# First four projection blocks of a hybrid decoder layer as float32 products of x times G, with rstd and the shift applied at eviction

## Chip, cores and metric

The kernel runs on one core of a Trainium2 chip. The metric is the device time of one execution in microseconds (us); lower is better. Engines are named as in the profile: PE is TensorE (matrix products; PEld its weight loads), DVE is VectorE, ACT is ScalarE, POOL is GpSimd, SP is SyncE. SP and POOL issue the transfers from and to HBM here.

## What is computed

One decoder layer over 2048 positions of width 1024. The part that matters here is the start: the modulation from the condition c, the modulated RMS norm, and the first columns of the combined input projection.

```python
cond = jax.nn.silu(c)
mod = (cond @ w_ada[l] + b_ada[l])[:, None, :]
sh1, sc1, g1, sh2, sc2, g2 = jnp.split(mod, N_MOD, axis=-1)

h = rms_norm(x, norm1_g[l]) * (1 + sc1) + sh1
proj = h @ w_in[l]
gq, gk, gv, gr, glr, aq, ak, av = jnp.split(proj, split_at, axis=-1)
```

Behind it come a chunked gated linear attention (from gq, gk, gv, gr, glr), a dilated softmax attention (from aq, ak, av), the output projection with a gated residual, and a second sub-layer with an up-projection, a causal convolution of width 3, a SwiGLU and a down-projection. All inputs are float32.

With G = norm1_g * (1 + sc1) and rstd the reciprocal root of the mean square of a position, h = x * G * rstd + sh1. G and sh1 belong to a column of x, rstd to a position. So h @ w = rstd * ((x * G) @ w) + sh1 @ w, where the last term is one number per output column.

## The kernel before

**Layout.** Positions are worked in four chunks (NCH) of T = 512. Within a chunk, activations lie transposed: 8 tiles (KD) of 128 channels by 512 positions. A block of weights w_ch is 128 x 1024: eight 128 x 128 pieces, one per k.

**Products.** Most products are "split": both operands are cut into a rounded part (hi) and the rest (lo), of type float32r, and `mm3` (L298) makes three products per piece: hi by hi (L304), hi of the weights by lo (L305), lo of the weights by hi (L306). Weights are loaded raw and split by `wslot` (L229): a cast on ACT (L238) gives hi, a subtraction on DVE (L239) gives lo. The raw tiles have two buffers, hi and lo four each.

**The start** (`run`, L1080). `ada_setup` loads c and the tables and makes silu(c) in `cond` (up to a factor of 2). `load_x(0)` loads the eight tiles of x. Sums of squares (L424, L429, L1091) go through a product with a matrix of ones (L443, plain float32), and L445 and L446 make rstd. The loop at L1096 then does, for each k: load scale block KD + k and shift block k of w_ada (L356; each 128 x 1024, in one or two pieces); for k < 4 load and split one of the blocks in FIRST = (0, 1, 2, 3); multiply each w_ada block with cond and sum it along its row (L360), which gives 128 values of `mod`; turn a scale into a column of G1 (L369); make one piece of the normalised input h0 by `norm_mod1`: x * G * rstd (L463, DVE), plus shift with rounding to hi (L465, ACT), and the rest as lo (L467, DVE). After the loop the four blocks are multiplied with `mm3` for each block and k (L1110 to L1112) into four PSUM tiles `done[b]`. These come from the pool `psg`, which has four.

**What follows.** `proj(0)` goes through ORDER0: g0 to g3 evict the four done blocks (`glaqk`, L518: ACT copies from PSUM with a factor, L521, then a store); the next entry, V0, is the first other work on TensorE (`av(0)`, L559, its products at L579 of 272 columns, L304 to L306 in the rows). A planner (`plan`, L248) lists all later weight blocks in order of use; `weights` (L287) loads and splits them up to three ahead. From there TensorE's work is a single stream: projections of four chunks, then the mixing of chunk c beside the up- and down-projections.

**What sets the order.** Each engine works its own queue in order. The program is written in the order above; the scheduler may place an instruction of an engine ahead of others that it doesn't depend on, and it does so at the start. Transfers of the start are issued by SP (`dq` while `planned` is false), later ones by POOL. `tie` and `after` add a dependence of a load on an instruction by hand. Tiles with a tag and a number of buffers make a load wait until the buffer's last reader is done.

Of the kernel before, what the change touches and what calls it, by code (L numbers as in the profile page):

```python
# [19 lines left out]
P = 128  # L20
T = 512
NCH = 4
KD = 8
# [4 lines left out]
FIRST = (0, 1, 2, 3)  # L28
# [84 lines left out]


def along(a, na, b, nb):

    acc = 0.0
    done = object()
    for _ in b:
        acc += na / nb  # L120
        while acc >= 1.0:
            acc -= 1.0
            if next(a, done) is done:
                acc = -1e9
        yield
    for _ in a:
        pass


def chain(*gs):  # L130
    for g in gs:
        yield from g


class K:
# [90 lines left out]
                y=d(f"y{c}", [8, P, T]), x1=d(f"x1{c}", [8, P, T])))  # L226


    def wslot(self, src, n=1024, spare=None):  # L229
        nc = self.nc  # L230
        raw = self.wraw.tile([P, 1088], F32, name="wraw")
        self.dq.dma_start(raw[:, :n], src)  # L232
        if spare is None:
            hi = self.whi.tile([P, 1088], F32R, name="whi")
            lo = self.wlo.tile([P, 1088], F32R, name="wlo")
        else:
            hi, lo = spare[:, 0:1024], spare[:, 1024:2048]
        nc.scalar.copy(hi[:, :n], raw[:, :n])  # L238
        nc.vector.tensor_tensor(lo[:, :n], raw[:, :n], hi[:, :n].bitcast(F32), op=ALU.subtract)  # L239
        return hi, lo  # L240

    def wblock(self, src, k, m, spare=None):
        hi, lo = self.wslot(src, k * m, spare)
        vh = hi[:, :k * m].rearrange("p (k m) -> p k m", k=k)
        vl = lo[:, :k * m].rearrange("p (k m) -> p k m", k=k)
        return [(vh[:, i], vl[:, i]) for i in range(k)]
# [96 lines left out]
    def soon(self, inst, n=20):  # L343
# [4 lines left out]
                break  # L348
        self.tc.add_manual_dep(inst.ins, mm.ins.name, mybir.DependencyInfo(mybir.DependencyClass.Sync, mybir.DependencyReason.DATA))

    def ada(self, b, raws):

        nc = self.nc
        n = 1024 // len(raws)
        for i, raw in enumerate(raws):
            ld = nc.sync.dma_start(raw, self.A["w_ada"][b][:, i * n:(i + 1) * n])  # L356
        yield
        m = self.mod[:, b:b + 1]
        for i, raw in enumerate(raws):
            self.last = nc.vector.tensor_tensor_reduce(raw, raw, self.cond[:, i * n:(i + 1) * n], 0.5, m if i else self.ba[:, b:b + 1], ALU.mult, ALU.add, m)  # L360
        self.ada_end(b)

    def ada_end(self, b):
# [107 lines left out]
    def proj(self, c, hs, hook=None, done=()):  # L471
        nc, A, D = self.nc, self.A, self.D[c]
# [3 lines left out]
        def stage(tag=None):  # L476
            if tag:
                return self.up.tile([P, T], F32, name="stg", tag=tag)
            return self.xp.tile([P, T], F32, name="stg", tag="x")

        def chan(b):
            w = self.weights("w_ch", b)
            ps = self.pg()
            self.mm3(ps, w, hs)
            return ps
# [30 lines left out]
            yield  # L516

        def glaqk(b):  # L518
            ps = done[b] if b in done else chan(b)
            s = stage()  # L520
            nc.scalar.activation(s, ps, AF.Copy, scale=0.125 if b < 2 else 1.0)  # L521
            self.dq.dma_start(D["gq" if b < 2 else "gk"][b % 2], s)
            yield

# [68 lines left out]
        def stores(g):  # L593

            for i, _ in enumerate(g):
                if late and i == 0:
                    next(late.pop(), None)
                yield

        ops = dict(W=wide, V=av, g=glaqk, q=qk)  # L600
        order = ORDER if c else ORDER0
        if put_off:
# [477 lines left out]
    def run(self):  # L1080
        self.ada_setup()
        self.scratch()
        self.x1, self.h2, self.tail = {}, {}, ()
        self.planned = False
        xs = self.load_x(0)
        acc = None
        for k in range(5):
            acc = self.square(acc, xs[k])
        sqs = [self.tmp.tile([P, T], F32, name="sq", bufs=3) for _ in range(5, KD)]
        for sq, x in zip(sqs, xs[5:]):  # L1090
            self.nc.scalar.activation(sq, x, AF.Square)  # L1091
        rstd = {0: self.norm_end(acc, more=sqs)}
        h0, ws, done = [], {}, {b: self.pg() for b in FIRST}
        spare = self.at.tile([P, 2048], F32R, name="w0", tag="kt", bufs=2)
        ring = self.at.tile([P, 2048], F32, name="ring", tag="kt", bufs=2)
        for k in range(KD):  # L1096
            big = [self.at.tile([P, 1024], F32, name="wada", tag="big", bufs=4)]
            pair = [self.gp.tile([P, T], F32, name="wada", tag=t) for t in ("ghi", "glo")] if k < 5 else [ring[:, (k - 5) * 1024:(k - 4) * 1024] if k < 7 else self.at.tile([P, 1024], F32, name="wada", tag="v4", bufs=1)]
            gs = [self.ada(KD + k, big), self.ada(k, pair)]
            for g in gs:  # L1100
                next(g)
            if k < len(FIRST):
                b = FIRST[k]
                ws[b] = self.wblock(self.A["w_ch"][b], KD, P, spare if k == 3 else None)
            for g in gs:
                next(g, None)
            if k == GATE:
                self.gate_ins = self.last
            h0.append(self.norm_mod1(xs[k], k, rstd[0], self.G1, self.mod[:, 0:8]))
        for b in FIRST:  # L1110
            for k in range(KD):
                self.mm3(done[b], ws[b][k:k + 1], h0[k:k + 1], k == 0, True)  # L1112
        self.consts()

        def src(c):
            def f(k):
                t = self.tmp.tile([P, T], F32, name="sq", bufs=3)
                ld = self.dq.dma_start(t, self.A["xT"][c, k])
                if c == 1:
                    self.after(ld)  # L1120
                return t
            return f

        self.wleft, self.wready, self.wpos = list(self.plan()), [], 0
        self.planned = True
        hs = [h0]

        def begin(c):
            hs.append(self.norm_mod(src(c), rstd[c], self.G1, self.mod[:, 0:8]))

        def proj(c):
            yield from self.proj(c, hs.pop(), (lambda: begin(c + 1)) if c < 3 else None, () if c else done)

        def stats(c):

            acc = None
            xs = [src(c)(0)]
            yield
            for k in range(KD):
                if k + 1 < KD:  # L1140
                    xs.append(src(c)(k + 1))
                yield
# [79 lines left out]
```

## Time and profile before

| what | us |
|---|---|
| median of 3 runs | 2595.93 |
| lowest, highest | 2593.44, 2597.0 |
| the profiled execution | 2592.85 |
| its span | 2591.1 |
| TensorE busy in the span | 2552.5 |
| DVE, ACT, POOL busy | 1930.3, 1276.8, 443.5 |

The profiled execution is one of its own; its span is the time from its first to its last instruction, and 1.75 us lie around it. Rows of the profile give the line, the engine, the operation, the tile written and the tiles read, the shape, and the count. In the rows of products, "128*128" is the stationary operand and "128x512" the streamed one; a row says f32 for float32 and float32r operands alike. A product's recorded length overlaps the next one's, so the cost of a product in a row of products is the distance of their starts.

### The profile page before, as it was taken

Reading aid. Unit: us, or ns where it says so; the run is one execution under the profiler, and the core shown is the slowest. Engines: PE = TensorE matmul, PEld = TensorE weight load, DVE = VectorE, ACT = ScalarE, POOL = GpSimd, SP = SyncE. Lnnn points to the kernel's source line nnn. Section 1 sums busy time; section 2 is a strip of 40 time slices with the busy share of each in tenths; the row PEclk is TensorE's granted clock in tenths of the full one; section 3 lists DMA queues with packets and bytes.
Section 4 is the critical chain, followed back from the end, with each engine's and each line's share of the span. In section 5 each row is a group of like instructions: output and inputs, shape, how many; then the busy total and the mean of one; then the engine's idle time right before and its main releaser. Section 6 shows DMA issues by size and latency. Waiting matters only on the chain.

```text
span 2591.1 us, 46836 instructions
## 1 busy us (share of the span) xinstructions
PE 2552.5 (99%) x18142; PEld 2099.2 (81%) x18142; DVE 1930.3 (74%) x4091; ACT 1276.8 (49%) x2626; POOL 443.5 (17%) x816
## 2 busy tenths in 40 slices
PE   6999999999999999999999999999999999999999
PEld 4888888788788888887888888878888888788887
DVE  8678877867688777677977777689777775766665
ACT  4556655766464544454545545346444553433332
POOL 2343432323210000022000000310000003100001
PEclk8999999999999999999999999999999999999999
DMA  8776764756532333355334343743443435422222
GB/s 316 245 235 221 233 214 167 237 178 210 213 111 95 123 129 129 124 197 184 108 110 133 125 131 125 253 139 114 125 145 125 141 102 191 155 98 98 98 97 83
DMA packets 163810, 404.93 MB, mean 156 GB/s; under 512 B 19154, under 2 KB 61572, under 8 KB 162308
## 3 DMA queue, kind: packets, MB, share of 16 engines
q0 software_dynamic: 88128, 308.59, 35.0%
q1 hardware_dynamic: 75460, 93.35, 11.4%
q8 instruction: 143, 2.34, 0.4%
q14 instruction: 79, 0.65, 0.1%
HBM read 338.95 MB, written 62.91 MB: 155 GB/s over the span
## 4 chain that ended last, share of the span: by engine, by line
PE 78%; issue 1%; DVE 1%; DMA 0%; ACT 0%; POOL 0%; POOLq 0%; DVEq 0%; ACTq 0%
PE psg L304 22%; PE psg L305 22%; PE psg L306 22%; PE psa L849 2%; PE psa L829 2%; PE psa L953 2%; PE psa L679 1%; PE psa L948 1%; PE psa L864 0%; PE psa L752 0%; PE psa L751 0%; PE psa L968 0%; PE psa L756 0%; PE psa L778 0%; DVE sq L463 0%
## 5 line engine op out<-in xcount | busy, mean ns | idle before, releaser
L304 PE MATMUL psg<-hhi,whi 128*128 128x512 f32 x1992 | 780.3, 395 | 10.2 <-ACT hhi L465 5.8
L305 PE MATMUL psg<-hlo,whi 128*128 128x512 f32 x1992 | 782.6, 394 | 6.4 <-DVE hlo L467 6.2
L306 PE MATMUL psg<-hhi,wlo 128*128 128x512 f32 x1992 | 780.0, 392 | 0.7 <-DVE wlo L239 0.7
L238 ACT CAST whi<-wraw 128x1024 fp32r<-128x1024 f32 (+1 forms) x391 | 410.4, 1051 | 471.2 <-PE psg L305 367.8
L239 DVE TENSOR_TENSOR wlo<-wraw,whi 128x1024 fp32r<-128x1024 f32 (+1 forms) x391 | 478.4, 1224 | 185.4 <-ACT whi L238 179.7
L304 PEld LDWEIGHTS psg<-hhi,whi 128*128 128x128 f32 x1992 | 374.3, 188 | 95.8 <-ACT hhi L465 9.8
L305 PEld LDWEIGHTS psg<-hlo,whi 128*128 128x128 f32 x1992 | 375.3, 188 | 85.9 <-DVE hlo L467 8.9
L306 PEld LDWEIGHTS psg<-hhi,wlo 128*128 128x128 f32 x1992 | 375.4, 188 | 80.5 <-issue 1.7
L304 PE MATMUL psg<-ghi,whi 128*128 128x512 f32 x744 | 295.0, 398 | 0.1
L305 PE MATMUL psg<-glo,whi 128*128 128x512 f32 x744 | 292.3, 393 | 0.9 <-DVE glo L998 0.9
L306 PE MATMUL psg<-ghi,wlo 128*128 128x512 f32 x744 | 291.5, 392 | 0.7 <-DVE wlo L239 0.7
L232 POOL DMA_DIRECT2D wraw<-in_w_up_dram x176 | 93.2, 530 | 983.0 <-DVE wlo L239 863.6
L1072 DVE SCALAR_TENSOR_TENSOR x<-psg,mod,x 128x512 f32<-128x512 f32 x192 | 143.4, 749 | 118.1 <-PE psg L306 115.5
L304 PE MATMUL psg<-whi,hhi 128*128 128x512 f32 (+2 forms) x512 | 171.4, 342 | 2.2 <-ACT stg L548 2.1
L306 PE MATMUL psg<-whi,hlo 128*128 128x512 f32 (+2 forms) x512 | 172.8, 341 | 0.0
L305 PE MATMUL psg<-wlo,hhi 128*128 128x512 f32 (+2 forms) x512 | 172.6, 339 | 0.1
L304 PEld LDWEIGHTS psg<-ghi,whi 128*128 128x128 f32 x744 | 139.5, 188 | 34.5 <-issue 5.3
L306 PEld LDWEIGHTS psg<-ghi,wlo 128*128 128x128 f32 x744 | 139.7, 188 | 30.6 <-DVE wlo L239 1.1
L305 PEld LDWEIGHTS psg<-glo,whi 128*128 128x128 f32 x744 | 139.8, 188 | 30.3 <-issue 1.9
L839 ACT ACTIVATE big<-big,nm 128x256 f32<-128x256 f32 (+1 forms) x256 | 122.4, 480 | 33.3 <-DVE nm L854 33.2
L1027 ACT ACTIVATE y<-psg,tables_sb 128x512 f32<-128x512 f32 x176 | 135.8, 774 | 4.5 <-PE psg L306 3.3
L1028 DVE SCALAR_TENSOR_TENSOR y<-psg,tables_sb,y 128x511 f32<-128x511 f32 x176 | 131.0, 745 | 3.7 <-ACT y L1027 3.6
(253 smaller groups left out, 3618.5 us busy)
## 6 DMA issues: line engine op xcount, KB each, us to landing
wraw<-in_w_up_dram POOLq DMA_DIRECT2D x176, 512.0 KB, 3.5
wraw<-in_w_down_dram POOLq DMA_DIRECT2D x88, 512.0 KB, 3.5
wraw<-in_w_ch_dram POOLq DMA_DIRECT2D x44, 512.0 KB, 4.2
v<-v SPq DMA_DIRECT2D x68, 256.0 KB, 5.4
wada<-in_w_ada_dram POOLq DMA_DIRECT2D x64, 256.0 KB, 4.9
wraw<-in_w_tokw_dram POOLq DMA_DIRECT2D x32, 512.0 KB, 4.2
wraw<-in_w_out_dram POOLq DMA_DIRECT2D x32, 512.0 KB, 4.4
sq<-in_xT_dram POOLq DMA_DIRECT2D x48, 256.0 KB, 4.6
```

The costliest lines, as they stand in the source:

```text
L232: self.dq.dma_start(raw[:, :n], src)
L238: nc.scalar.copy(hi[:, :n], raw[:, :n])
L239: nc.vector.tensor_tensor(lo[:, :n], raw[:, :n], hi[:, :n].bitcast(F32), op=ALU.subtract)
L304: nc.tensor.matmul(ps, wh, hh, start=first and k == 0, stop=False, skip_group_check=shared)
L305: nc.tensor.matmul(ps, wh, hl, start=False, stop=False, skip_group_check=shared)
L306: self.lastmm = nc.tensor.matmul(ps, wl, hh, start=False, stop=k == n - 1, skip_group_check=shared)
L829: nc.tensor.matmul(at(i, hh, z), q[H[hh], i * P:(i + 1) * P], key(H[hh], i, z), start=True, stop=True, skip_group_check=True)
L839: nc.scalar.activation(t[:, lo:hi], t[:, lo:hi], AF.Exp, bias=nm[:, hh, g, i:i + 1], scale=2.0 ** -(h + 1), accum_out=dn[:, hh, g, i:i + 1])
L849: nc.tensor.transpose(ps[:n, i * P:(i + 1) * P], part(S[hh], i), self.C("id"))
L1027: nc.scalar.activation(y, ps, AF.Identity, bias=self.cb[:, b:b + 1], scale=self.cw[:, 2, b:b + 1])
L1028: nc.vector.scalar_tensor_tensor(y[:, 1:], ps[:, :T - 1], self.cw[:, 1, b:b + 1], y[:, 1:], op0=ALU.mult, op1=ALU.add)
L1072: nc.vector.scalar_tensor_tensor(x1, ps, self.mod[:, 40 + cb:41 + cb], x1, op0=ALU.mult, op1=ALU.add)
```

## The change

The first four blocks are multiplied in plain float32, without a split, with g = x * G as the streamed operand (ACT, scale = G1 column) and the raw weights. The loop goes over k outside and the blocks inside. rstd is multiplied in at the eviction (DVE, from PSUM), and the shift's part, sh1 @ w, comes from 32 products of one column each into one PSUM tile `ps`; ACT adds it as a bias. The normalised input h0 is still made, for all later blocks.

The loads are issued in another order: the first scale block, then x, then a w block and a scale block in turn, the other scale blocks, and then all shift blocks. The tiles that they land in change with that. The first two weight loads of the planner are tied to the last scale step (`held`).

```diff
-    def wslot(self, src, n=1024, spare=None):
+    def wslot(self, src, n=1024):
...
-        self.dq.dma_start(raw[:, :n], src)
...
+        ld = self.dq.dma_start(raw[:, :n], src)
+        if self.held:
+            self.tie(ld, self.held.pop())
+        hi = self.whi.tile([P, 1088], F32R, name="whi")
+        lo = self.wlo.tile([P, 1088], F32R, name="wlo")
...
         def glaqk(b):
-            ps = done[b] if b in done else chan(b)
             s = stage()
-            nc.scalar.activation(s, ps, AF.Copy, scale=0.125 if b < 2 else 1.0)
+            scale = 0.125 if b < 2 else 1.0
+            if b in done:
+                nc.vector.tensor_tensor(s, done[b], self.rstd0, op=ALU.mult)
+                nc.scalar.activation(s, s, AF.Identity, scale=scale, bias=self.shw[:, b:b + 1])
+            else:
+                nc.scalar.activation(s, chan(b), AF.Copy, scale=scale)
...
+        scales = [self.ada_load(KD, [raw("wada")])]
         xs = self.load_x(0)
+        two = self.at.tile([P, 2048], F32, name="w0", tag="kt", bufs=2)
+        ws = [two[:, 0:1024], two[:, 1024:2048]] + [self.whi.tile([P, 1088], F32, name="whi")[:, 0:1024] for _ in range(2)]
+        for k in range(1, KD):
+            if k <= len(FIRST):
+                nc.sync.dma_start(ws[k - 1], self.A["w_ch"][FIRST[k - 1]])
+            scales.append(self.ada_load(KD + k, [raw("wada")]))
...
+            shifts.append(self.ada_load(k, raws))
...
         for k in range(KD):
-            big = [self.at.tile([P, 1024], F32, name="wada", tag="big", bufs=4)]
...
-                ws[b] = self.wblock(self.A["w_ch"][b], KD, P, spare if k == 3 else None)
...
+            self.ada(*scales[k])
+            g = self.at.tile([P, T], F32, name="xg", tag=("pt", "s16", "stage")[(k > 4) + (k > 6)], bufs=5 if k < 5 else 2)
+            nc.scalar.activation(g, xs[k], AF.Copy, scale=self.G1[:, k:k + 1])
+            for i, b in enumerate(FIRST):
+                self.lastmm = nc.tensor.matmul(done[b], ws[i][:, k * P:(k + 1) * P], g, start=k == 0, stop=k == KD - 1, skip_group_check=True)
+        self.hist.append((4 * KD, self.lastmm))
+        self.held = [self.last, self.last]
+        h0 = []
+        for k in range(KD):
+            self.ada(*shifts[k])
             if k == GATE:
                 self.gate_ins = self.last
             h0.append(self.norm_mod1(xs[k], k, rstd[0], self.G1, self.mod[:, 0:8]))
-        for b in FIRST:
+        ps = self.pa()
+        for i in range(len(FIRST)):
             for k in range(KD):
-                self.mm3(done[b], ws[b][k:k + 1], h0[k:k + 1], k == 0, True)
+                nc.tensor.matmul(ps[:, i:i + 1], ws[i][:, k * P:(k + 1) * P], self.mod[:, k:k + 1], start=k == 0, stop=k == KD - 1)
+        self.shw = self.const.tile([P, 4], F32, name="shw")
+        nc.vector.tensor_scalar(self.shw[:, 0:2], ps[:, 0:2], 0.125, None, op0=ALU.mult)
+        nc.vector.tensor_copy(self.shw[:, 2:4], ps[:, 2:4])
         self.consts()
```

More of the change, by code (lines that the diff above doesn't have):

```diff
@@ L226, in scratch @@
                 y=d(f"y{c}", [8, P, T]), x1=d(f"x1{c}", [8, P, T])))
-    def wslot(self, src, n=1024, spare=None):
+    def wslot(self, src, n=1024):
         nc = self.nc
         raw = self.wraw.tile([P, 1088], F32, name="wraw")
-        self.dq.dma_start(raw[:, :n], src)
[L233 to L237, printed above, removed]
+        ld = self.dq.dma_start(raw[:, :n], src)
[3 more added lines that the diff above has]
+        lo = self.wlo.tile([P, 1088], F32R, name="wlo")
         nc.scalar.copy(hi[:, :n], raw[:, :n])
@@ L240, in wslot, with wblock @@
         return hi, lo
-    def wblock(self, src, k, m, spare=None):
-        hi, lo = self.wslot(src, k * m, spare)
+    def wblock(self, src, k, m):
+        hi, lo = self.wslot(src, k * m)
         vh = hi[:, :k * m].rearrange("p (k m) -> p k m", k=k)
@@ L349, in soon, with ada_load, ada @@
         self.tc.add_manual_dep(inst.ins, mm.ins.name, mybir.DependencyInfo(mybir.DependencyClass.Sync, mybir.DependencyReason.DATA))
-    def ada(self, b, raws):
-        nc = self.nc
+    def ada_load(self, b, raws):
         n = 1024 // len(raws)
         for i, raw in enumerate(raws):
-            ld = nc.sync.dma_start(raw, self.A["w_ada"][b][:, i * n:(i + 1) * n])
-        yield
+            self.nc.sync.dma_start(raw, self.A["w_ada"][b][:, i * n:(i + 1) * n])
+        return b, raws
+    def ada(self, b, raws):
+        n = 1024 // len(raws)
         m = self.mod[:, b:b + 1]
         for i, raw in enumerate(raws):
-            self.last = nc.vector.tensor_tensor_reduce(raw, raw, self.cond[:, i * n:(i + 1) * n], 0.5, m if i else self.ba[:, b:b + 1], ALU.mult, ALU.add, m)
+            self.last = self.nc.vector.tensor_tensor_reduce(raw, raw, self.cond[:, i * n:(i + 1) * n], 0.5, m if i else self.ba[:, b:b + 1], ALU.mult, ALU.add, m)
         self.ada_end(b)
@@ L1084, in run @@
         self.planned = False
+        self.held = []
+        nc = self.nc
+        raw = lambda n: self.at.tile([P, 1024], F32, name=n, tag="big", bufs=4)
+        scales = [self.ada_load(KD, [raw("wada")])]
         xs = self.load_x(0)
+        two = self.at.tile([P, 2048], F32, name="w0", tag="kt", bufs=2)
[4 more added lines that the diff above has]
+            scales.append(self.ada_load(KD + k, [raw("wada")]))
+        ring = self.at.tile([P, 2048], F32, name="ring", tag="kt", bufs=2)
+        shifts = []
+        for k in range(KD):
+            if k < 2:
+                raws = [self.wlo.tile([P, 1088], F32, name="wlo")[:, 0:1024]]
+            elif k < 5:
+                raws = [self.gp.tile([P, T], F32, name="wada", tag=t) for t in ("ghi", "glo")]
+            else:
+                raws = [ring[:, (k - 5) * 1024:(k - 4) * 1024] if k < 7 else self.at.tile([P, 1024], F32, name="wada", tag="v4", bufs=1)]
+            shifts.append(self.ada_load(k, raws))
+        done = {b: self.pg() for b in FIRST}
         acc = None
@@ L1090, in run @@
         for sq, x in zip(sqs, xs[5:]):
-            self.nc.scalar.activation(sq, x, AF.Square)
+            nc.scalar.activation(sq, x, AF.Square)
         rstd = {0: self.norm_end(acc, more=sqs)}
-        h0, ws, done = [], {}, {b: self.pg() for b in FIRST}
-        spare = self.at.tile([P, 2048], F32R, name="w0", tag="kt", bufs=2)
-        ring = self.at.tile([P, 2048], F32, name="ring", tag="kt", bufs=2)
+        self.rstd0 = rstd[0]
         for k in range(KD):
-            big = [self.at.tile([P, 1024], F32, name="wada", tag="big", bufs=4)]
[L1098 to L1103, printed above, removed]
-                ws[b] = self.wblock(self.A["w_ch"][b], KD, P, spare if k == 3 else None)
-            for g in gs:
-                next(g, None)
+            self.ada(*scales[k])
[6 more added lines that the diff above has]
+        h0 = []
+        for k in range(KD):
+            self.ada(*shifts[k])
             if k == GATE:
```

## Prediction

> **What bounds the kernel now.** I read the page first, then the table by stretches of the first 150 us, then TensorE's waits there, then single rows. The page:
>
> ```profile
> span 2591.1 us, 46836 instructions
> PE 2552.5 (99%) x18142; PEld 2099.2 (81%) x18142; DVE 1930.3 (74%) x4091; ACT 1276.8 (49%) x2626; POOL 443.5 (17%) x816
> ```
>
> TensorE (PE) is idle for only 2591.1 - 2552.5 = 38.6 us; at 99% busy it sets the end. So a change pays only if it takes work from TensorE or closes one of its gaps. The stretches show where the gaps are (columns: stretch, its length, busy time of the engines, granted clock, DMA share, GB/s):
>
> ```profile
> 0.00:10.90 10.90, 0.00 (x0) 0.00 (x0) 5.47 (x12) 6.97 (x9) 0.21 (x4) 1.00 0.84 296
> 10.90:15.25 4.35, 4.34 (x5) 1.85 (x6) 3.54 (x9) 1.79 (x3) 0.08 (x1) 1.00 1.03 400
> 15.25:22.08 6.83, 2.23 (x6) 0.68 (x4) 6.28 (x12) 4.24 (x6) 1.14 (x2) 1.00 1.04 399
> 22.08:28.90 6.82, 4.63 (x10) 3.13 (x10) 6.82 (x16) 0.27 (x1) 0.00 (x0) 0.50 1.04 398
> 28.90:32.30 3.40, 1.11 (x4) 0.59 (x4) 3.40 (x10) 1.49 (x2) 0.00 (x0) 1.00 1.04 412
> 32.30:39.10 6.80, 5.82 (x14) 4.14 (x13) 6.80 (x11) 2.38 (x3) 0.53 (x1) 0.50 0.97 363
> 39.15:48.10 8.95, 8.32 (x37) 6.55 (x35) 8.95 (x18) 2.56 (x3) 2.49 (x5) 1.00 0.37 112
> 48.10:55.90 7.80, 7.56 (x32) 5.93 (x33) 4.47 (x8) 4.20 (x6) 2.79 (x6) 1.00 0.89 333
> 55.90:150.00 94.10, 94.10 (x506) 81.92 (x507) 63.59 (x99) 53.24 (x84) 35.97 (x65) 1.00 0.73 247
> PE psg L305 <- DVE hlo L467: 4.7, 3, 2.9
> PE psg L304 <- ACT hhi L465: 4.4, 2, 3.6
> ```
>
> From 55.90 us on TensorE has no gap. Before that it idles, and twice, for about 6.8 us, it runs at a granted clock of 0.50. DVE is full from 22.08 to 48.10, and TensorE waits for what DVE makes (the last two rows, from the view of waits over 0 to 55.9 us). So the start is bound by loads and DVE, the rest by TensorE, and what counts is one moment: when the product after the four first blocks starts, the first of V0 (L579). Everything behind it is back to back.
>
> ```profile
> 42.32 0.39 PE L304 MATMUL psg<-hhi,w 128*128 128x512 f32 x1
> 42.55 0.39 PE L305 MATMUL psg<-hlo,w 128*128 128x512 f32 x1
> ...
> 55.41 0.39 PE L306 MATMUL psg<-hhi,w 128*128 128x512 f32 x1
> 55.90 0.39 PE L304 MATMUL psg<-whi,hhi 128*128 128x272 f32 x1
> ```
>
> V0 starts at 55.90. I work out when it starts after the change; the difference is the gain.
>
> **The change part by part.** Removed from TensorE: 4 blocks x 8 x 3 split products at 42.55 - 42.32 = 0.23 us each at full clock, 96 x 0.23 = 22 us. Added: 32 float32 products of 512 columns, and 32 of one column for the shift. Their prices:
>
> ```profile
> L443 PE MATMUL psa<-rstd,ones 128*128 128x512 f32 x10 | 5.1, 592 | 0.0
> 711.06 1.02 PE L443 MATMUL psa<-rstd,ones 128*128 128x512 f32 x2
> ...
> 436.65 0.30 PE L920 MATMUL psa<-xm,consts_sb 128*128 128x32 f32 x2
> 436.79 0.53 PE L849 MATMUL psa<-consts_sb,big 128*128 128x128 f32 x3
> ...
> 256.08 0.39 PE L751 MATMUL psa<-state,pt 128*128 128x128 f32 x2
> 256.30 0.39 PE L752 MATMUL psa<-big,sbd 128*128 128x128 f32 x2
> ```
>
> A float32 product is two records here. L443's two take 1.02 us and one lasts 0.592, so they start 0.43 apart, and the product costs 2 x 0.43 = 0.86 us. 32 x 0.86 = 27.5 us: the work on TensorE grows by 5.5 us. What is bought with it is an early start, since these products need neither rstd nor the shift nor a split.
>
> The one-column product is not in the trace. Above, the nearest is L920, 32 columns against the same 128 x 128 weights: from its start to the next one, 436.79 - 436.65 = 0.14 us. For 128 columns (L751 to L752) it is 0.22. Below, its two records alone start 0.30 us minus about 0.27 (the length of the last) = 0.03 apart, 0.06 for both. So 32 of them cost 1.8 to 7.0 us; I take L920's 0.14, the nearest in size, 4.5 us. A gain is excluded: they are new work on a full engine.
> The Trainium skill (TensorE: Matmul & The Clock Gate, section on LDWEIGHTS) gives a weight load as its columns divided by 1.2 per ns, whatever is streamed: 107 ns for 128, twice per float32 product. By that rule the 32 would cost an estimated 6.8 us; the 0.14 of L920 speaks against it, but no run here shows such products in a row.
>
> When the work can start follows from the loads:
>
> ```profile
> 0.00:12.00 12.00, 1.09 (x2) 0.58 (x3) 6.24 (x13) 7.79 (x11) 0.21 (x4) 1.00 0.85 304
> 12.00:36.00 24.00, 13.94 (x29) 7.49 (x28) 22.96 (x48) 8.52 (x11) 1.30 (x3) 0.78 1.04 403
> wada<-in_w_ada_dram SPq DMA_DIRECT2D x9, 512.0 KB, 8.0
> x<-in_xT_dram SPq DMA_DIRECT2D x8, 256.0 KB, 4.9
> wraw<-in_w_ch_dram SPq DMA_DIRECT2D x4, 512.0 KB, 8.8
> cond<-in_c_dram SPq DMA_DIRECT2D x1, 512.0 KB, 4.3
> tables_sb<-in_tables_dram SPq DMA_DIRECT2D x1, 123.0 KB
> ```
>
> By 12 us 12 x 304 GB/s = 3.65 MB have landed, then 0.40 MB per us; the queues are full up to 36 us, so the order of issue decides. A block of 512 KB is 0.52 MB, 1.3 us. One scale block now goes ahead of x, which is 1.3 us later. The sums of squares (L443, four float32 products) started at 10.90, so now at 12.2. Behind x: w0 lands at 12.4 (3.8 MB: cond, tables, one scale block, x, w0), then scale and w in turn, so w1 at 15.0, w2 at 17.6, w3 at 20.2 and the last scale at 25.5. The order of work is k outside, block inside: up to 20.2 us TensorE has the four sums of squares and the products with w0 to w2, first at about half speed (below); from then on products wait for TensorE, not the other way round. The last scale needs some 2.5 us on DVE and ACT (its block of L360 took about 1.3, rows below; x times G is 512 columns) and is ready at 28, with TensorE still busy for 17 us. I see no gap.
>
> The clock at the start, from TensorE's weight loads and products:
>
> ```profile
> 11.92 0.34 PEld L443 LDWEIGHTS psa<-sq,ones 128*128 128x128 f32 x1 [0.52 <-ACT sq L1091]
> 12.78 0.34 PEld L443 LDWEIGHTS psa<-sq,ones 128*128 128x128 f32 x1 [0.52 <-issue]
> ...
> 15.73 1.02 PE L443 MATMUL psa<-rstd,ones 128*128 128x512 f32 x2
> ...
> 20.37 0.73 PE L304 MATMUL psg<-hhi,whi 128*128 128x512 f32 x2 [3.62 <-ACT hhi L465]
> ```
>
> L443's first records stood 12.78 - 11.92 = 0.86 apart instead of 0.43, until about 15.25, when the 0.43 of the last pair begins: 4.35 us at half speed. The same again costs 4.35 / 2 = 2.2 us. The sum for TensorE: 12.2 + 2.2 + (4 + 32) x 0.86 = 45.4 us for the end of the four blocks, + 4.5 = 49.9 us for the start of V0.
>
> Does V0 then find its data? It needs h0, which DVE makes:
>
> ```profile
> 48.75 1.64 DVE L467 SCALAR_TENSOR_TENSOR hlo<-x,mod,hhi 128x512 fp32r<-128x512 f32 x2
> ...
> L360 DVE CUSTOM_DVE_ANT_0 wada<-wada,cond,tables_sb 128x1024 f32<-128x1024 f32 (+1 forms) x14 | 15.0, 1092 | 0.3 <-DMA wada<-in_w_ada_dram 0.3
> L467 DVE SCALAR_TENSOR_TENSOR hlo<-x,mod,hhi 128x512 fp32r<-128x512 f32 x8 | 6.0, 751 | 0.1
> L463 DVE SCALAR_TENSOR_TENSOR x<-x,G,rstd 128x512 f32<-128x512 f32 x8 | 6.0, 749 | 0.0
> L239 DVE TENSOR_TENSOR wlo<-wraw,whi 128x1024 fp32r<-128x1024 f32 (+1 forms) x4 | 5.0, 1240 | 0.9 <-ACT whi L238 0.9
> L429 DVE TENSOR_TENSOR rstd<-rstd,sq 128x512 f32<-128x512 f32 x4 | 2.8, 692 | 1.2 <-ACT sq L424 0.9
> ```
>
> Before, h0 was complete at 48.75 + 1.64 = 50.4. DVE loses four splits (4 x 1.24 = 5.0 us), which gives 45.4 if it stays full. From 27 us, with the scales done, there remain eight shift steps (the 14 of L360's first row at 1.09 are whole and half blocks; about 1.3 per block, 10.4), eight L467 (6.0) and two splits for V0 (2.5): 46 if all eight L463 fit into the wait for the scales, up to 52 if none does. V0 walks through the eight pieces of h0 in 24 products of 272 columns, 272 / 512 x 0.23 = 0.12 us each, so its last piece may come 2.6 us after its start; both ends just do. But the one-column products stand in front of V0 and need shift 7. It comes about 1.5 us (ACT's rounding of the piece and an L467 of 0.75) before the end of h0, at 44.5 to 50.5. At the near end it is hidden; at the far end TensorE waits (a rival below). DVE filled its waits before (it made L463 of later pieces between other work), so I take the near end.
>
> The other edits. The eviction of blocks 0 to 3: a product with rstd on DVE (0.69, as L429's row of that size) before ACT's step. The four PSUM tiles are all that the pool has, so V0 waits for the first of these DVE steps. The one-column products (4.5 us) cover it; without that cover it costs 0.7 us. Behind it on DVE stand h0's pieces (if the step is put ahead of them: the third rival). ACT's second step waits for the shift product; behind it on ACT stand casts of weights needed several us later. The four casts and splits of w0 to w3 go, but TensorE no longer waits for them, so nothing is booked twice. V0's two weight loads now wait for the last scale step, 27 us, and land by about 33, far ahead of 49.9. Shift loads stand behind all scale loads on SP's queue; with V0's two blocks, each about as big as a w block, 14.3 MB have landed by then, at 12 + (14.3 - 3.65) / 0.40 = 38.6; DVE reaches it later anyway. None of these is on the path.
>
> So V0 starts at about 50.0 instead of 55.9: 5.9 us less, 0.23%. The profiled execution took 2592.85 us (span 2591.1), this gives 2587.0; the three runs had a median of 2595.93 (2593.44 to 2597.0), so I forecast 2590.0. A measurement of this kernel tells about 0.2%, 5.2 us, from no change.
>
> **The rivals.**
> 1. The shift's products cost more: dear, or late. At 0.22 each (L751) V0 starts at 52.4; with shift 7 at 50.5 and 25 products of 0.14 behind it, at 54.0. Gain 1.9 to 3.5 us, 2592.4 to 2594.0: not to be told from no change. For it: DVE was full for 26 us. Against: DVE has 5.0 us less to do and waits to fill. Chance 0.27. By the Trainium skill's rule on weight loads (above) V0 would start at an estimated 52.2.
> 2. The clock falls once more. Before, a gap of 3.62 us (from 16.75 to the product at 20.37) was followed by a granted clock of 0.50 for 6.8 us (row of 22.08). If TensorE idles so long between 12 and 20 us (w2 and w3 late) or at shift 7, one such stretch costs 3.4 us and the gap itself: gain -1 to 2.5 us, 2593.4 to 2597. Against: by the sum float32 work covers that time. Chance 0.15. The Trainium skill (TensorE: Matmul & The Clock Gate, Part 1) ties the fall to an idle window of about 3.4 us; the gap of 3.62 us agrees.
> 3. DVE's evictions stand too early in its queue. They wait for the end of the four blocks, 45.4, and DVE works in order. If whatever ordered the queue expected that end at some 28 us (as it would with float32 products at the split ones' price), all eight shift steps and pieces would stand behind: 45.4 + 2.8 for the evictions + about 16 = 64, V0 at 62, 6 us slower, 2602. It turns into a loss when over 10 us of DVE's work stands behind (five of eight steps). For it: nothing in this trace; L521 stood behind h0 before. Chance 0.08.
> 4. The edit's effect is smaller than the order of later work varies, or it doesn't do what it says: about 2595 to 2597. Chance 0.03.
>
> **How the numbers follow.** The forecast has 0.47; its own range goes from products at 0.06 (V0 at 47.2, gain 8.7) to the mark of 5.2 us: 2587.2 to 2590.7. Faster: this 0.47 and 0.03 of rival 1's best end, 0.50. Slower: rival 3 and a rest of the second, 0.09. Same: 0.41. The range goes from 2586 (the best end, less about a us for the spread of runs) to 2597 (the end of rival 2), and leaves rival 3 out.
>
> **What would show it.** In the changed profile: L443 at about 12.2 us; records of 0.43 apart from about 16.5 to 45; no 0.50 in the granted clock after that; 64 one-column records within 4.5 us; V0 at 50.0 with no gap over 1 us before it; h0's last piece on DVE between 45 and 52, evictions behind it. It is wrong if TensorE shows a gap over 2 us between 12 and 50, or if V0 starts before 47 or after 53.

## The result and the profile after

The changed kernel takes 2602.91 us (median of 8 runs, 2600.44 to 2605.53), the kernel before, run beside it, 2596.47 (8 runs, 2593.44 to 2598.94). The ratio is 1.0026, with a 95% interval of 1.0015 to 1.0037: slower by a quarter of a per cent. The profiled execution of the changed kernel took 2603.07 us, against 2592.85 of the one before. In the changed code `mm3` has L303 to L305, the sums L445, the steps of scales and shifts L362, x times G L1125, the float32 products L1127, the one-column products L1139 and the evictions L524.

The head of the page of the changed kernel:

```profile
span 2601.3 us, 46890 instructions
PE 2569.3 (99%) x18174; PEld 2106.4 (81%) x18174; DVE 1928.4 (74%) x4089; ACT 1278.5 (49%) x2630; POOL 444.3 (17%) x816
```

TensorE's idle time went down, from 38.6 us to 2601.3 - 2569.3 = 32.0, as the change means it to. But its busy time went up by 2569.3 - 2552.5 = 16.8 us, where 5.5 us of added float32 work and 4.5 us for the shift were booked. Busy time that nobody ordered is a sign to look at the granted clock. TensorE's rows in order of time, changed kernel, up to V0 (start, length, operation, count, and in brackets the wait before it):

```profile
13.51 5.14 PE L445 MATMUL psa<-sq,ones 128*128 128x512 f32 x6 [13.51 <-ACT sq L1119]
...
19.34 3.60 PE L1127 MATMUL psg<-xg,w 128*128 128x512 f32 x8
22.77 1.88 PE L1127 MATMUL psg<-xg,whi 128*128 128x512 f32 x4
...
33.07 0.50 PE L1139 MATMUL psa<-mod,w 128*128 128x1 f32 x4
33.44 1.96 PE L1127 MATMUL psg<-xg,w 128*128 128x512 f32 x4
35.24 1.88 PE L1127 MATMUL psg<-xg,whi 128*128 128x512 f32 x4
36.95 1.18 PE L1139 MATMUL psa<-mod,w 128*128 128x1 f32 x8
39.39 0.38 PE L1139 MATMUL psa<-mod,w 128*128 128x1 f32 x2 [1.26 <-DVE mod L362]
40.59 2.70 PE L1139 MATMUL psa<-mod,w 128*128 128x1 f32 x18 [0.82 <-DVE mod L362]
43.15 4.41 PE L1139 MATMUL psa<-mod,whi 128*128 128x1 f32 x20
47.42 3.76 PE L1127 MATMUL psg<-xg,w 128*128 128x512 f32 x4
50.97 2.54 PE L1127 MATMUL psg<-xg,whi 128*128 128x512 f32 x4
...
60.22 1.40 PE L1139 MATMUL psa<-mod,whi 128*128 128x1 f32 x12
61.48 0.37 PE L303 MATMUL psg<-whi,hhi 128*128 128x272 f32 x1
```

V0 starts at 61.48, not at 49.9 as forecast, and 5.58 us later than the 55.90 of before. From 36.95 to 47.42 there is no float32 product of 512 columns, only one-column products. 20 of the 32 long ones (40 records) are done by then, the last 12 come behind. The same span in the table by stretches (length, busy time of PE, PEld, DVE, ACT, POOL, granted clock, DMA share, GB/s):

```profile
18.16:42.05 23.89, 21.74 (x70) 11.21 (x70) 21.63 (x42) 7.70 (x11) 2.15 (x5) 1.00 0.90 344
42.06:52.29 10.23, 10.23 (x33) 7.53 (x33) 9.75 (x19) 7.48 (x11) 3.17 (x6) 0.50 0.92 326
52.30:61.47 9.17, 9.17 (x31) 4.68 (x30) 5.85 (x9) 3.63 (x7) 3.20 (x6) 1.00 0.59 202
61.48:150.00 88.52, 88.52 (x484) 77.28 (x484) 57.85 (x92) 48.63 (x77) 31.36 (x55) 1.00 0.69 233
...
36.95:42.06 5.11, 2.96 (x24) 2.70 (x23) 5.11 (x9) 0.72 (x1) 2.17 (x5) 1.00 0.40 125
```

From V0 up to 150 us there is no gap, as before. Ahead of V0, 5.11 us of one-column products with waits are followed by 10.23 us at a granted clock of 0.50, which cost 5.1 us of work.

Why the last 12 products came so late is in the rows of SP's queue and of DVE and ACT. SP's first (the loads of L354 are scales and shifts, told apart by their tiles: `wlo`, `ring` and the six halves are shifts):

```profile
15.42 0.33 SPq L354 DMA_DIRECT2D wada<-in_w_ada_dram  x1
16.66 0.33 SPq L354 DMA_DIRECT2D wlo<-in_w_ada_dram  x1
17.93 6.73 SPq L354 DMA_DIRECT2D wada<-in_w_ada_dram  x6
25.61 1.61 SPq L354 DMA_DIRECT2D ring<-in_w_ada_dram  x2
27.57 2.42 SPq L354 DMA_DIRECT2D wada<-in_w_ada_dram  x4
```

The load at 15.42 is scale 4. The next in the program are scales 5 to 7; SP issues six more shift blocks first, and the scales in the group at 27.57. Scale tiles have four buffers (the tag "big"), and scales 5 to 7 need one that an earlier scale step has left. The shifts lie in tiles that were free. So the scheduler put them ahead. It is the compiled order that holds the scales back and not a wait on the chip: the step of scale 1 had read its buffer by 17.95, and between 13 and 31 us SP waited for DVE only 0.3 us in all. DVE's queue got the same order, as its rows and those of ACT show:

```profile
41.12 1.28 DVE L362 CUSTOM_DVE_ANT_0 wada<-wada,cond,tables_sb 128x1024 f32<-128x1024 f32 x1
42.33 1.28 DVE L362 CUSTOM_DVE_ANT_0 wada<-wada,cond,tables_sb 128x1024 f32<-128x1024 f32 x1
43.60 1.28 DVE L362 CUSTOM_DVE_ANT_0 wada<-wada,cond,tables_sb 128x1024 f32<-128x1024 f32 x1
```

```profile
43.72 0.72 ACT L1125 ACTIVATE xg<-x,G 128x512 f32<-128x512 f32 x1 [5.50 <-DVE G L371]
44.99 0.72 ACT L1125 ACTIVATE xg<-x,G 128x512 f32<-128x512 f32 x1 [0.55 <-DVE G L371]
46.28 0.71 ACT L1125 ACTIVATE xg<-x,G 128x512 f32<-128x512 f32 x1
```

These are the last three scale steps and the last three x times G. Twelve products need them (three k by four blocks), and by 43.72 the one-column products already stand in TensorE's queue in front of those twelve.

So two things of the change meet: the order of the loads makes a gap, and one-column products fill it. How much is whose, the runs have to say.

### The profile page after: what moved, and what is told of

Read it like the earlier page. It is cut to its first block, busy times and chain, and to the rows that moved or that the text cites. A ratio compares the mean times of both kernels' runs of the same rounds, so it can differ in the third digit from the quotient of the medians.

```text
span 2601.3 us, 46890 instructions
## 1 busy us (share of the span) xinstructions
PE 2569.3 (99%) x18174; PEld 2106.4 (81%) x18174; DVE 1928.4 (74%) x4089; ACT 1278.5 (49%) x2630; POOL 444.3 (17%) x816
## 4 chain that ended last, share of the span: by engine, by line
PE 77%; issue 1%; DVE 1%; DMA 0%; ACT 0%; POOL 0%; POOLq 0%; DVEq 0%; ACTq 0%
PE psg L303 22%; PE psg L304 22%; PE psg L305 22%; PE psa L855 2%; PE psa L835 2%; PE psa L959 2%; PE psa L685 1%; PE psa L954 1%; PE psa L870 0%; PE psa L758 0%; PE psa L757 0%; PE psa L974 0%; PE psa L762 0%; DVE sq L465 0%; PE psa L784 0%
## 5 line engine op out<-in xcount | busy, mean ns | idle before, releaser
L303 PE MATMUL psg<-hhi,whi 128*128 128x512 f32 x1968 | 772.1, 395 | 4.0 <-DVE x L1078 1.6
L304 PE MATMUL psg<-hlo,whi 128*128 128x512 f32 x1968 | 772.0, 393 | 2.0 <-DVE hlo L469 1.8
L305 PE MATMUL psg<-hhi,wlo 128*128 128x512 f32 x1968 | 769.8, 392 | 0.7 <-DVE wlo L238 0.7
L303 PEld LDWEIGHTS psg<-hhi,whi 128*128 128x128 f32 x1968 | 369.7, 188 | 86.2 <-issue 4.2
L305 PEld LDWEIGHTS psg<-hhi,wlo 128*128 128x128 f32 x1968 | 370.3, 188 | 79.1 <-issue 1.7
L303 PE MATMUL psg<-ghi,whi 128*128 128x512 f32 x744 | 296.6, 400 | 0.0
L305 PE MATMUL psg<-ghi,wlo 128*128 128x512 f32 x744 | 292.5, 393 | 0.0
L303 PE MATMUL psg<-whi,hhi 128*128 128x512 f32 (+2 forms) x512 | 171.5, 342 | 2.1 <-ACT stg L554 2.1
L305 PE MATMUL psg<-whi,hlo 128*128 128x512 f32 (+2 forms) x512 | 172.8, 341 | 0.0
L303 PEld LDWEIGHTS psg<-ghi,whi 128*128 128x128 f32 x744 | 140.4, 189 | 34.3 <-issue 5.3
L305 PEld LDWEIGHTS psg<-ghi,wlo 128*128 128x128 f32 x744 | 140.2, 188 | 29.4 <-issue 0.7
```

Source lines behind the costliest of these rows:

```text
L303: nc.tensor.matmul(ps, wh, hh, start=first and k == 0, stop=False, skip_group_check=shared)
L304: nc.tensor.matmul(ps, wh, hl, start=False, stop=False, skip_group_check=shared)
L305: self.lastmm = nc.tensor.matmul(ps, wl, hh, start=False, stop=k == n - 1, skip_group_check=shared)
```

## The experiments

Two theories stood at the start. A: the order of the loads (scales 5 to 7 behind the shifts) makes a gap, and the fall of the clock follows from it. B: the one-column products themselves are what costs. In the tables below V0 and spans are those of a profiled execution, medians are over the runs of one kernel. The first four kernels ran on one chip beside 31 runs of the kernel before (median 2595.83), the later ones on two other chips, each beside runs of before of its own.

**Without the shift's products.** The kernel leaves out the shift's part of the first four blocks.

```diff
-                nc.tensor.matmul(ps[:, i:i + 1], ws[i][:, k * P:(k + 1) * P], self.mod[:, k:k + 1], start=k == 0, stop=k == KD - 1)
...
+        nc.vector.memset(self.shw, 0.0)
```

> The changed kernel without its 32 one-column products: the shift's part of the first four blocks is left out (their bias is zero). Theory A (order and clock: the last three scale loads wait for tiles in use and are overtaken by the shift loads, so the last 12 float32 products can't start before about 45 us, and the clock falls while TensorE has only one-column products or nothing): the products are mostly in time that is idle anyway; the last 12 float32 products still start at 45 to 47 us with a granted clock of 0.50 in between, V0 starts at 59 to 60.3 instead of 61.48, time 1 to 2 us below the changed kernel. Theory B (price: the added work on TensorE, 5.5 us for float32 and 6.7 us for one column at 0.21 us each, is what was lost): 6.7 us go, V0 at about 55, time 6 to 7 us below the changed kernel.

Measured: 2596.94 (10 runs), ratio to before 1.0003 [0.9994, 1.0013]; V0 at 57.14. TensorE's rows, then the stretch behind the gap:

```profile
44.80 3.78 PE L1127 MATMUL psg<-xg,w 128*128 128x512 f32 x4 [7.83 <-ACT xg L1125]
...
57.14 0.69 PE L303 MATMUL psg<-whi,hhi 128*128 128x272 f32 x1
```

```profile
44.80:49.50 4.70, 4.70 (x6) 2.12 (x7) 4.64 (x11) 4.20 (x8) 1.60 (x3) 0.50 1.00 368
```

The gap is there without them, 7.83 us of real waiting for x times G, and the clock falls too, to 0.50 behind it. That is A's picture. But V0 lies 4.3 us earlier than with them, where A had put it at 59 to 60.3 and B at 55: their price is larger than A held, about halfway. The time is 6.0 us below the changed kernel, which is what B had expected (6 to 7). Both have a part.

**The shift's products 128 columns wide.** The column of the shift is read 128 times, so that each product streams 128 columns instead of one; nothing else changes.

```diff
-                nc.tensor.matmul(ps[:, i:i + 1], ws[i][:, k * P:(k + 1) * P], self.mod[:, k:k + 1], start=k == 0, stop=k == KD - 1)
+                nc.tensor.matmul(ps[:, i * P:(i + 1) * P], ws[i][:, k * P:(k + 1) * P], self.mod[:, k:k + 1].to_broadcast([P, P]), start=k == 0, stop=k == KD - 1, skip_group_check=True)
```

> The changed kernel with the shift's column repeated 128 times, so that each shift product streams 128 columns instead of one; by the row of L751 such a product costs 0.22 us, against 0.21 measured for one column. Theory A: the same order and the same length of these products, but the granted clock stays 1.00 from 18 us on; the last 12 float32 products run at 0.86 us each, V0 at 56.5 to 57.5, time about 4 to 5 us below the changed kernel. Rival: the clock fell because of the two waits of 1.26 and 0.82 us, not because of the columns: it falls again, V0 at 61 to 62, time as the changed kernel.

Measured: 2599.48 (10 runs), ratio 1.0013 [1.0004, 1.0023]; V0 at 56.34. Its rows of TensorE, then of the table by stretches:

```profile
42.55 2.40 PE L1139 MATMUL psa<-mod,whi 128*128 128x128 f32 x20
44.78 1.88 PE L1127 MATMUL psg<-xg,w 128*128 128x512 f32 x4
...
56.34 0.37 PE L303 MATMUL psg<-whi,hhi 128*128 128x272 f32 x1
```

```profile
36.80:44.78 7.98, 6.10 (x49) 5.57 (x48) 7.98 (x17) 1.44 (x2) 2.65 (x5) 1.00 0.63 213
44.78:56.34 11.56, 11.56 (x38) 5.82 (x37) 11.09 (x18) 8.77 (x13) 4.92 (x10) 1.00 0.84 281
```

The order and the waits are those of the changed kernel, but in the profiled execution the clock holds 1.00 from 18 us to V0, and V0 comes 61.48 - 56.34 = 5.14 us earlier: the 5.1 us that half the clock cost. More columns cost no more time, since 20 records take 44.78 - 42.55 = 2.23 us, 0.112 each. So here it was not the waiting alone that brought the clock down, but that the products between the waits stream a single column. This execution is the fastest of the ten, and the median is only 3.4 us below the changed kernel, where 4 to 5 were expected. The mean granted clock of every run is on record (to 0.001): on average these ten spent 16.6 us at half clock, the eight of the changed kernel 20.8. So with the waits left in, the fall may still have come in some of them; no trace shows which.

**All scales in tiles of their own.** The eight scale blocks get tiles that are free at the start, the last shifts the recycled ones.

```diff
+        ring = self.at.tile([P, 2048], F32, name="ring", tag="kt", bufs=2)
...
-            scales.append(self.ada_load(KD + k, [raw("wada")]))
+            scales.append(self.ada_load(KD + k, [raw("wada") if k < 4 else ring[:, (k - 4) * 1024:(k - 3) * 1024] if k < 6 else self.at.tile([P, 1024], F32, name="wada", tag="v4", bufs=1) if k < 7 else self.wlo.tile([P, 1088], F32, name="wlo")[:, 0:1024]]))
```

> The changed kernel with tiles handed out the other way: all eight scale blocks get tiles that are free at the start, four of the shift blocks get recycled ones. All work is as in the changed kernel. Theory A: all scale loads go ahead of the shift loads, the 32 float32 products run without a gap from about 18.5 to 47 us, the one-column products follow (6.7 us), V0 at 53 to 54.5 (up to 57 if the clock falls during the one-column products), time 5 to 8 us below the changed kernel and 0 to 2.5 below the kernel before. Theory B: no more than 2 us below the changed kernel, still slower than before.

Measured: 2598.63 (10 runs), ratio 1.0009 [1.0000, 1.0019]; V0 at 55.19. The time misses the expectation, 4.3 us below the changed kernel where A had 5 to 8. Rows of TensorE, then stretches:

```profile
46.13 3.40 PE L1139 MATMUL psa<-mod,w 128*128 128x1 f32 x30
49.40 5.93 PE L1139 MATMUL psa<-mod,whi 128*128 128x1 f32 x32
55.19 0.57 PE L303 MATMUL psg<-whi,hhi 128*128 128x272 f32 x1
```

```profile
46.13:50.55 4.42, 4.42 (x42) 4.42 (x40) 4.42 (x7) 1.07 (x2) 2.62 (x5) 1.00 1.00 357
50.55:55.19 4.64, 4.64 (x23) 4.64 (x24) 3.53 (x8) 1.35 (x3) 1.64 (x2) 0.50 0.59 213
55.19:60.79 5.60, 5.60 (x26) 5.60 (x27) 4.55 (x9) 5.41 (x8) 3.77 (x7) 0.50 0.86 282
```

The gap is gone: all 32 long products run in one piece up to 46.13. And the clock falls nevertheless, 4.42 us into a stretch in which both PE and its weight loads are busy for all of the time by the profile. This is the sharpest row of the study. There is no wait here, from 16.42 on; one-column products alone bring the clock down, and 5.60 of the 10.24 us at half of it lie behind V0, where they cost another 2.8 us. So A is half right. The order does cost: V0 comes 6.3 us earlier, 3.5 if the 2.8 us behind it are counted (in the profiled execution, 2594.28, the fastest of the ten). But the fall of the clock doesn't need the gap, and with the order mended it stays.

**Both edits together.**

> Both edits, own tiles and 128 columns. Theory A: as the kernel with own tiles, but the granted clock stays 1.00 from 18 us on, so V0 at 53 to 54 and the time equal to or up to 3 us below that of own tiles alone, 2 us below the kernel before. Theory B: as the changed kernel.

Measured: 2594.38 (10 runs), ratio 0.9996 [0.9987, 1.0006]; V0 at 54.32 and the clock at 1.00 from 18.8 to 657 us. TensorE's rows:

```profile
47.48 3.51 PE L1139 MATMUL psa<-mod,w 128*128 128x128 f32 x30
50.83 3.73 PE L1139 MATMUL psa<-mod,whi 128*128 128x128 f32 x32
54.32 0.37 PE L303 MATMUL psg<-whi,hhi 128*128 128x272 f32 x1
```

The four corners, V0 in us:

| | one column | 128 columns |
|---|---|---|
| tiles of the change | 61.48 | 56.34 |
| scales in tiles of their own | 55.19 (+ 2.8 behind V0) | 54.32 |

The time with both edits is 4.3 us below that of own tiles alone, where up to 3 were expected. Either edit alone leaves a loss in the median (own tiles at the edge of what can be told), both together bring the kernel back to the time of before. That the wider products hold the clock goes for more than this one execution: the ten runs with own tiles spent 18.7 us on average at half clock, these ten 8.8, and the difference of 9.9 is about the 10.24 of that one fall. The lower right corner isn't better by the full 2.3 us that half the clock costs ahead of V0 in the lower left one, because in this execution the slow start lasted longer: L445's last pair stood at 18.93, against 17.58 there.

**POOL's early loads.** In the changed kernel POOL issues two loads of later modulation blocks (0.52 MB) at 1.28 us, ahead of x; before, they were issued at 15.17 and 20.61, each after a wait for a step of L360 that read its buffer. Here they are held back, the rest is the changed kernel.

```diff
-                if not n:
+                if n < 5:
                     self.after(ld)
```

> The changed kernel with POOL's two early loads for the later modulation (L383, issued at 1.28 us) held back until the shift steps, nothing else. Theory A (these 0.52 MB go ahead of x and explain why the first product came at 13.51 instead of the forecast 12.2): first product at 12.2, but the last three scale loads are still overtaken and the clock still falls, so V0 comes only 0.5 to 2 us earlier than 61.48 and the time is 0 to 2 us below the changed kernel. Rival (the late start of the first product has other causes): first product at 13.5, no change.

Measured, beside 21 runs of before with a median of 2595.23: 2607.29 (4 runs), ratio 1.0044 [1.0030, 1.0058]. The first product starts at 12.00 instead of 13.51, as expected. V0 comes at 62.97 and the time lies 4.4 us above the changed kernel, where I expected both to be lower: a miss. Rows of TensorE and of DVE:

```profile
41.64 5.69 PE L1139 MATMUL psa<-mod,whi 128*128 128x1 f32 x26
47.19 3.76 PE L1127 MATMUL psg<-xg,w 128*128 128x512 f32 x4
...
62.97 0.36 PE L303 MATMUL psg<-whi,hhi 128*128 128x272 f32 x1 [2.86 <-ACT sq L439]
```

```profile
60.73 1.49 DVE L431 TENSOR_TENSOR rstd<-rstd,sq 128x512 f32<-128x512 f32 x2 [4.10 <-ACT sq L426]
62.14 1.28 DVE L524 TENSOR_TENSOR stg<-psg,rstd 128x512 f32<-128x512 f32 x2
```

The gap still ends with the late scales (47.19, against 47.42), with six more one-column records in front of the last products, at half the clock. But six fewer stand behind them, and the half clock ends at 50.85 instead of 52.29, so TensorE is done with everything ahead of V0 at 62.97 - 2.86 = 60.11, 1.4 us earlier than in the changed kernel: the gain was there, as expected. A new wait of 2.86 us takes it away. V0 writes into a tile that an eviction L524 has to empty; the evictions stand in DVE's queue behind sums of squares for the next chunk (L431), which wait for later loads, and the first ends at 62.82. The row names a cast on ACT (L439) that stands behind L431 too and ends at 62.88; which of the two came last for V0, the trace doesn't tell. Behind this wait the clock falls once more, at 64.5.

**Two variants on mended tiles.** The one streams 64 columns; the other adds the held loads, takes x and the blocks alternately and puts the float32 products ahead of the sums of squares.

> The kernel with own tiles and with shift products of 64 columns, between one column (the clock fell at 50.5 us for 10.24 us) and 128 (it held). The length of these products should stay about 0.21 us. If the clock goes by how much of the time columns are streamed, 64 columns stream 4 x 64 / 2.4 GHz-steps, half of the 128-column time, and either outcome is open: held, V0 at 53 to 54.5 and the time as with 128 columns (2594 to 2595); or fallen, V0 at 55 and V0's first products at half speed, time 2598 to 2599. I expect it to hold (0.6).

> A version meant to be better than both: own tiles, 128 columns, POOL's two loads held back, and the first float32 products ahead of the sums of squares, with loads in the order s0 x0 w0 x1 s1 x2 x3 w1 and so on. Theory A (what counts is when V0 starts, and that is start + 36 float32 products + shift products at full clock): first product at 9.5 to 10.5 us, the four blocks done at 43 to 44, V0 at 49.5 to 52 (the last pieces of h0 from DVE may hold it at 51), no 0.50 in the granted clock after 20 us; time 4 to 6 us below the kernel before, 2590 to 2592. Rival (DVE is the bound of the start: it is full from 26 to 54 us in the version with own tiles and 128 columns): V0 at 53 to 54.5, time 2594 to 2595.

Measured: with 64 columns 2596.43 (10 runs), ratio 1.0006 [0.9997, 1.0016], V0 at 53.46, clock at 1.00 until 652 us: 64 columns held it as 128 did, in the execution that was profiled. V0 is as expected, the time 1.4 us above what was expected for it. The other order: 2596.76 (11 runs), ratio 1.0005 [0.9996, 1.0014], V0 at 52.59, but the first product only at 12.42, where 9.5 to 10.5 was expected, and the time is above both expectations: a miss. The first scale step stood on DVE behind two sums of squares (L431 from 8.72) and began at 10.12. The gain of V0 doesn't show in the time; most of it was given back to the clock further on (below).

**The best version**: tiles of their own, 128 columns, POOL's loads held.

> Own tiles, shift products of 128 columns, and POOL's two early loads held back; the order of the first products as in the changed kernel. Theory A (time = start of V0 + 2535 us + half the time that the clock is at 0.50 behind V0): first product at 12.0, V0 at 52.5 to 53, no 0.50 before 400 us; time 1.5 us below own tiles with 128 columns, if the falls behind V0 are as many: 2592 to 2594. Rival (the version with early products shows that an earlier V0 is given back later): V0 at 52.5 to 53 and the time again 2595 to 2597.

Measured: 2594.43 (11 runs), before beside it 2596.42 (15 runs), ratio 0.9991 [0.9982, 1.0000]. V0 at 52.55, the first product at 12.04:

```profile
49.06 3.73 PE L1139 MATMUL psa<-mod,whi 128*128 128x128 f32 x32
52.55 0.37 PE L303 MATMUL psg<-whi,hhi 128*128 128x272 f32 x1
```

With the gap gone the held loads pay: V0 lies 1.8 us ahead of the same kernel without them, and 0.9 ahead of the one with 64 columns, whose slow start happened to end earlier. The time, 2594.43, lies between the two expectations. The version is well ahead of the change as made, and against the kernel before at the edge of what can be told: 2 us in the median.

**Both kernels once more**, one execution each, for how the clock's later falls spread.

> The kernel before, profiled once more. If the later falls of the clock are a matter of how the clock's windows lie in that run, V0 starts at 55.9 within 1.5 us again (its own two half-clock windows may move it), and one to three stretches of 3.4 or 6.8 us at 0.50 appear behind it, near 503, 655, 1730 or 2230 us, where the first profile had none; the time fits V0 + 2535 us + half of them within 2 us. If they belong to the changed kernel's code, none appears.

> The changed kernel, profiled once more: V0 at 60 to 62 again with a fall of the clock between 40 and 53 us, which belongs to the order of its work; the later falls may lie elsewhere than at 660 and 2237 us, and the time fits V0 + 2535 us + half of the later ones within 2 us.

Measured: before 2595.88 with V0 at 56.38, after 2601.50 with V0 at 60.97, the clock down in the head at 40.9 for 10.2 us again. In the kernel before, the clock fell once behind V0 this time, at 656 us; in the changed one at 659 and 1737. So later falls are not peculiar to the changed kernel. The granted clock also falls far behind the head, in the mixing stages; two rows of the changed kernel, from the table by stretches:

```profile
659.90:666.60 6.70, 6.55 (x79) 5.03 (x78) 6.69 (x11) 2.81 (x7) 2.17 (x5) 0.50 1.04 385
2236.90:2240.20 3.30, 3.30 (x9) 2.52 (x9) 3.30 (x5) 0.72 (x1) 0.72 (x2) 0.50 0.34 132
```

Taking V0 and half of the time at half clock behind V0 from the span leaves nearly the same rest for every kernel:

| execution | span | V0 | half clock behind V0 | rest |
|---|---|---|---|---|
| before | 2591.1 | 55.90 | 0 | 2535.2 |
| before, again | 2594.1 | 56.38 | 3.41 | 2536.0 |
| after | 2601.3 | 61.48 | 10.24 | 2534.7 |
| after, again | 2599.7 | 60.97 | 10.24 | 2533.6 |
| no shift products | 2594.7 | 57.14 | 6.83 | 2534.2 |
| 128 columns | 2595.0 | 56.34 | 10.24 | 2533.5 |
| own tiles | 2592.5 | 55.19 | 5.60 | 2534.5 |
| own tiles, 64 columns | 2593.4 | 53.46 | 10.24 | 2534.9 |
| own tiles, 128 columns | 2595.3 | 54.32 | 6.83 | 2537.6 |
| the same, loads held | 2593.2 | 52.55 | 10.24 | 2535.5 |
| loads held alone | 2606.7 | 62.97 | 17.07 | 2535.2 |
| the other order | 2597.0 | 52.59 | 17.07 | 2535.8 |

The rest spreads over 4 us while V0 spreads over 10 and the last term over 8.5. So of the 10.2 us between the two executions that were compared line by line, 5.6 are V0 and 5.1 are falls far behind it. How many later falls there are changes from one execution to the next: none in the first of before, one window in the second.

The mean clocks on record say more about the medians. They give the mean time at half clock; from it I take off the falls in the head and the 0 to 2.7 us at the very end, as each kernel's profiles show them. What is left is an estimate of the half clock behind V0, and it assumes that the heads of the other runs were like the profiled one. Before: 22.1, 20.5 and 23.2 us at half clock (31, 21 and 15 runs), 13.7 in the head, so 4 to 7 behind V0. Changed: 20.8, of which 10.2 in the head, so about 8. So of the 6.4 us between the medians about 5 are V0 and about 1 the later falls. Own tiles with 64 columns, the other order, and the best version: 12.5, 12.7 and 13.2, none of it in the head, so 10 to 13. These three, with V0 2.4 to 3.4 us ahead of before, had 3 to 8 us more at half clock behind it, which is 1.5 to 4 us of time: much or all of the gain. Why an earlier V0 should meet more falls, these runs don't settle.

## Why the prediction was wrong

The start of V0 was the right moment to work out, and it came 11.6 us later than the sum's 49.9. What lies behind it isn't quite back to back, though: before, TensorE idled 16.7 of its 38.6 us behind V0, and there the clock falls in some executions, which moves the time by a few us. Step by step:

- **The first product at 12.2**: 13.51, 1.3 late. POOL's two loads went ahead of x; with them held it was 12.00. The sum followed SP's queue and forgot POOL's, whose two loads before had waited for steps on DVE and now waited for nothing.
- **Cold start, 2.2**: L445 ran from 13.51 to the full clock at 18.16, 4.65 / 2 = 2.3. Right.
- **A float32 product at 0.86**: eight records from 19.34 to 22.77 are 0.43 each, two per product. Right.
- **"Shift loads stand behind all scale loads on SP's queue … I see no gap."** This is the first of two steps that failed. The prediction took the program's order for the queue's. The last scale step was to be ready at 28; x times G of the last piece began at 46.28. The diff showed it: the scales have four buffers, one of which the start uses for another tile, and a load that must wait for a buffer can be overtaken by loads that need not. That brought two waits (2.1 us) and put one-column products where long ones should have been.
- **The one-column product at 0.14**: 0.22. With own tiles 30 records at full clock took (49.40 - 46.13) / 30 = 0.109 each, two per product. That is 32 x 0.22 = 7.0 us and not 4.5. The upper bound was right, the choice between the bounds wrong: L920's row was nearest in columns streamed, but TensorE's weight loads are busy for all of this stretch (4.42 of 4.42 us), and the width doesn't change the price (0.112 at 128). L920's product stands alone: the first of its two weight loads began at 436.43, while the product before it still ran, so its 0.14 holds only one. The Trainium skill (TensorE: Matmul & The Clock Gate, section on LDWEIGHTS) gives a rule by which such a load takes an estimated 107 ns: at full clock the 0.109 agrees. (The lower bound, 32 x 0.06, is 1.9 and not 1.8; nothing hangs on it.)
- **"No 0.50 in the granted clock after that"**: this is the second step that failed, and the dearest: 10.23 us of it from 42.06, 5.1 us of work, a term that the sum put at nothing. Rival 2 had the fall with a price of 3.4 us and tied it to an idle TensorE. The run with own tiles shows it without a wait.
- **DVE's evictions**: L524 ran only from 57.85, behind h0, so rival 3's mechanism did not happen, though its time, 2602, was met. A right number for another reason proves nothing; in the run with POOL's loads held the evictions stood too late in the queue, not too early, and V0 waited 2.86 us.

The sum from 49.9: 1.3 for the first product, 0.1 for the cold start, 2.5 for the price of the one-column products, 2.1 for two waits, 5.1 for the clock are 61.0. The 0.5 to the measured 61.48 is nearly all in the tails of the records ahead of the two waits: from 36.95 to 40.59 ten records and the waits take 3.64 us, and 10 x 0.109 + 2.1 is 3.2. The best version is the sum as forecast with the price alone put right: 49.9 + 2.5 = 52.4, measured 52.55. The chances failed in one more place: rivals 1 and 2 were treated as exclusive, 0.27 and 0.15, each ending at no change. Here both came from the same 32 one-column products, which were dear and brought the clock down, and they added up. Two losses of about 3 us with one trigger belong in one case, with the sum of both as its time.

## What to carry to other kernels

When loads are put in another order, go through the buffers of each tile before believing the order: a load into a recycled tile waits, and the issuing queue, and the engine behind it, may take the later ones first. Book tiny products by their weight loads, and don't let a stretch of several us of them stand on TensorE: widen what they stream, which here cost next to nothing (0.112 against 0.109 us a record), or spread them among long products (not tried here). And price rivals that share a trigger together.

## What the runs showed of the hardware

A stretch of one-column products counts for the clock like idling, though the profile shows TensorE as full: with own tiles the clock fell 4.42 us into it and stayed at 0.50 for 10.24 us. The same number of products with 64 or 128 columns held 1.00, at the same 0.11 us per record. All four profiled executions with one column show the fall ahead of V0, none of the five with 64 or 128. Where between 1 and 64 the border lies wasn't tried.

At half the clock the one-column record doubles: 20 of them from 43.15 to 47.42 in the changed kernel are 0.2135 each, against 0.109. So this price, in stretches where the weight loads are busy throughout, goes by the same clock.

Ahead of TensorE's last work, falls of the clock lasted 3.4, 6.8 or 10.2 us in all profiled executions, multiples of 3.41, and the stretch at full clock before the fall is one too: 18.16 to 42.06 in the changed kernel is 7 x 3.41, 16.42 to 50.55 with own tiles 10 x 3.41. The Trainium skill (TensorE: Matmul & The Clock Gate, Part 1) gives the clock's window as about 3.4 us, and the durations agree; that the window is running freely, as it says there, would let the number of later falls vary from one execution to the next as it did.
